# Expert tokens gathered from two rounded parts of the residual instead of three bf16 parts, with four experts in the first gather, in a hybrid decoder layer

## The chip, the cores and the metric

One core of one Trainium2 chip runs the whole layer. The metric is device time in microseconds (us), the median of 3 executions. The lower the better.

## What is computed

One layer: RMSNorm, a mixer (mLSTM heads and S5 groups), the residual x1 = x + mixer, and a mixture of experts, then a last RMSNorm. The change touches the passage from x1 to the experts:

```python
def hierarchical_moe(h, ...):               # h = rmsnorm(x1, norm_ffn_g), 256 tokens x 1024
    g_logits = (t @ rg_w) + rg_b            # 4 groups, top 1
    e_logits = (t @ re_w) + re_b            # 8 experts in that group, top 2
    ...
    for e in range(32):                     # 32 experts, 1024 -> 512 -> 1024
        ye = (silu(t @ w_gate[e]) * (t @ w_up[e])) @ w_down[e]
        y = y + combine[:, e:e + 1] * ye
```

All is float32. The weights of the 32 experts are 201 MB, read once.

## The kernel before

**Instruction order.** The schedule is written out by hand: each engine runs its instructions in the order of the program text, and waits only on semaphores. The engines are PE (TensorE), DVE (VectorE), ACT (ScalarE), POOL (GpSimd) and SP (SyncE, which here only issues DMAs).

**Expert weights.** `fetch(upto)` issues the next loads, 1 MB each (a quarter of the gate, up or down matrices of one pair of experts, 12 loads a pair, 192 in all, in the order of the list `order`). They go into 23 buffers (`NP` = 23, named `half0` to `half22`) that are reused in turn. Until the experts start, these buffers also hold the mixer's weights and scratch. Load number 22 (counted from 0) goes into `half5`, where x1 lies until the router has read it. Load 23 is the first that reuses a buffer of an expert: SP waits at it until the gate matmuls of pair 0 have gone through c = 0 to 3.

**From x1 to the first expert** (L1035 to L1097). x1 is finished in four PSUM pieces (128 tokens `b` by 512 columns `q`). `residual` copies each to SBUF, `squares` sums its squares, `transpose1` transposes it for the router, `logits` multiplies it with the router weights, and `choose` (9 small DVE operations) gives the mask `msk` of each token's two experts. `rank` multiplies the mask with a triangle of ones on PE, which numbers the tokens of each expert, and `onehots` turns the numbers into one-hot columns (`oh`), 64 places for each expert. `warm` issues matmuls whose results nobody reads. `parts_of_x` splits x1 into three bf16 tiles `xp` whose sum is x1; each piece costs two ACT and two DVE operations. `gather_first` multiplies the parts with the one-hots of experts 0 and 1 only, and `gains` scales the result into `xg`, the operand of the experts. In pair 0 (L1109 on) the gate matmuls (`wide`, L1014) follow. Between c = 3 and c = 4 come the factors, the count `cnt` of tokens for the largest expert, and the one-hots of experts 2 and 3, which are gathered after pair 0's up matmuls. Later `gather(range(4))` gathers four experts at a time, in the odd pairs 1 to 13.

**A pair**: gate (8 values of c), Silu on ACT, up (8 values), product on DVE, four transposes (L1152), down, and the scatter of the pair before into four PSUM banks. The last pair's down matrices come in ten smaller loads. At the end ten sums and scalings give the output (from L1202).

**Memory.** `mw`, `cst`, `Sc` and `xall` are tiles of their own. `cap` first holds the causal mask. Once its last reader is done, the final norm's gains are loaded into it on SP's queue (L748), and PE spreads them in pair 14 (L1147).

Of the kernel before, what the change touches and what calls it, by code (L numbers as in the profile page):

```python
# [19 lines left out]
P = 128  # L20
# [52 lines left out]
def tile_hymba(ctx, tc, x, norm_mix_g, w_in, conv_w, conv_b, i_bias, f_bias, mlstm_norm_g,  # L73
# [21 lines left out]
    xall = pool.tile([P, 3072], F32, name="xs")  # L95
    xs = cuts(xall, (2, 1024))[0]
    xp = cuts(xall.bitcast(BF16), (3, 2, 1024))[0]
    Y = pool.tile([P, 2, 512], F32R, name="Y")
    Sc = pool.tile([P, 2, 128], F32R, name="Sc")
    mw = pool.tile([P, 3840], F32, name="mw")  # L100
    ident = pool.tile([P, P], F32, name="ident")
    cst = pool.tile([P, 1584], F32, name="cst")
    PS = pp.tile([P, 8, 512], F32, name="psum")
    (g1, g2, gbias, mask8, mask2, dl16, dlt4, half_pi, neg_half, one, idx, ssq, en, rd, sq, sc, mgh, hb) = cuts(
        cst, 8, 8, 1, 8, 2, 16, 4, 1, 8, 1, 128, 2, (2, 4), (2, 4), (2, 4), (2, 4), 4, 4)
    (lg, gm, tv, msk, m12, rk, wt, el, es, pen, gw, w1, w2, r2, s2, cnt) = cuts(
        cst, (2, 40), (2, 8), (2, 8), (2, 32), (2, 2, 32), (2, 32), (2, 32), (2, 32), (2, 4), (2, 4), 2, 2, 2, 2, 2, 2,
        start=228)
    tri, ones, cap, rbias, rw, rTB, ldt0, sh, wp = cuts(
        cst, 128, 128, 128, 40, (8, 40), 80, 2, (2, 2), 2, start=752)  # L110
    oh = cuts(cst.bitcast(BF16), (2, 4, 64), start=2 * 1176)[0]

    rpt = cuts(cst.bitcast(BF16), (2, 3), start=2 * 1496)[0]
    rtmp, rp = cuts(cst, 2, 2, start=1500)
# [44 lines left out]
    va, pre, La, mr, R = cuts(mw, (2, 4, 129), (4, 256), 256, 256, (2, 4, 128))  # L159
    Gt, Bc, Mx = cuts(smB, 256, 256, 256)  # L160
    K4T, dd2 = cuts(mw, 512, (16, 2, 16))
    hh = cuts(mw, (2, 4, 129), start=2056)[0]
# [541 lines left out]
    zt = cuts(mw, (2, 256), start=3088)[0]  # L704
# [43 lines left out]
    SP.dma_start(cap[0:8], norm_final_g.rearrange("(c n) -> c n", c=8))  # L748
# [102 lines left out]

    x1 = cuts(half(5), (2, 1024))[0]
    LB = (2, 4)

# [48 lines left out]
    def rank(b):  # L903
        rp = PS[:, LB[b], 64:96]
        MM(rp, tri, msk[:, b], start=b == 0, stop=True, skip_group_check=True)
        yield
        STT(rk[:, b], rp, 1.0, msk[:, b], OP.add, OP.mult)
        yield
        onehots(0, (0, 1), (b,))
        yield  # L910
# [25 lines left out]

    def parts_of_factors():
        V.tensor_copy(rpt[:, :, 0], r2)
        TT(rtmp, r2, rpt[:, :, 0], OP.subtract)
        V.tensor_copy(rpt[:, :, 1], rtmp)  # L940
        TT(rpt[:, :, 2], rtmp, rpt[:, :, 1], OP.subtract)
# [3 lines left out]
    xg, act, aT, ow = cuts(mw, (8, 256), 512, (4, 128), (2, 2, 64))  # L945
# [3 lines left out]
    def gather_first(b, steps):  # L949

        for k, q in steps:
            for c in range(4):
                MM(PS[:, DN[q], 128 * c:128 * c + 128], xp[:, k, b, 4 * q + c::8],
                   oh[:, b, 0:2].rearrange("p e s -> p (e s)"), start=c == b == k == 0, stop=b == 1 and k == 2,
                   skip_group_check=True)
            if b and k == 2:
                gains(DN[q], slice(4 * q, 4 * q + 4), slice(0, 128))

    def factors(js, bk):

        at = PS[:, bk, 0:8].rearrange("p (j k) -> p j k", j=2)
        for n, j in enumerate(js):
            for b in range(2):
                MM(at[:, j, 0:3], oh[:, b, 2 * j:2 * j + 2].rearrange("p e s -> p (e s)"), rpt[:, b],
                   start=n == b == 0, stop=b == 1, skip_group_check=True)
        V.tensor_reduce(rp[:, js[0]:js[-1] + 1], at[:, js[0]:js[-1] + 1, 0:3], AX.X, OP.add)

    def gains(bk, cs, ss):
        n, m = cs.stop - cs.start, ss.stop - ss.start
        TT(xg[:, cs, ss], PS[:, bk, :].rearrange("p (c s) -> p c s", c=n), fr(g2[:, cs], (1, n), (0, m)), OP.mult)  # L970

    def onehots(e0, es, bs=(0, 1)):
# [5 lines left out]
    def gather(es):  # L978

        n = 8 // len(es)  # L980
        ss = slice(64 * es[0], 64 * es[-1] + 64)
        m = ss.stop - ss.start
        for f in range(8 // n):
            for c in range(n):
                for b in range(2):
                    for k in range(3):
                        MM(PS[:, DN[f % 2], m * c:m * c + m], xp[:, k, b, n * f + c::8],  # L987
                           oh[:, b].rearrange("p e s -> p (e s)")[:, ss], start=c == b == k == 0, stop=b == 1 and k == 2,
                           skip_group_check=True)
            gains(DN[f % 2], slice(n * f, n * f + n), ss)  # L990
# [45 lines left out]
    sqs, junk1 = cuts(mw, 1024, 512, start=2048)  # L1036
# [3 lines left out]
    next(part[0, 0])  # L1040
    next(part[0, 0])
# [12 lines left out]
    next(part[0, 1])  # L1054
    next(part[0, 1])
# [17 lines left out]
    fetch(NP)  # L1073
    next(part[1, 1])
    next(part[1, 0])
# [4 lines left out]
    logits(1, 1)  # L1080
    run(rank0)
    next(part[1, 1])
# [261 lines left out]
```

## Time and profile before

| what | value |
|---|---|
| median of 3 runs | 608.95 us (608.2 to 609.27) |
| time of the profiled execution | 607.72 us |
| its span | 606.0 us |
| PE busy | 585.0 us, 97% |
| DVE busy | 224.2 us, 37% |
| ACT busy | 127.3 us, 21% |
| POOL busy | 57.5 us, 9% |
| moved by DMA | 219.79 MB, 363 GB/s on average |

The span is the stretch from the first instruction to the last. The profiled execution's own time is 1.72 us longer than it. Busy time of PE is modelled and counts matmuls that overlap as one stretch. PEld is the loading of PE's stationary operand, which overlaps with PE. An f32 matmul shows as two records; an f32r one (f32 data, rounded, one pass) as one, and its weight loads are labelled f32.

### The profile page before, as it was taken

Reading aid. Unit: us, or ns where it says so; the run is one execution under the profiler, and the core shown is the slowest. Engines: PE = TensorE matmul, PEld = TensorE weight load, DVE = VectorE, ACT = ScalarE, POOL = GpSimd, SP = SyncE. Lnnn points to the kernel's source line nnn. Section 1 sums busy time; section 2 is a strip of 40 time slices with the busy share of each in tenths; the row PEclk is TensorE's granted clock in tenths of the full one; section 3 lists DMA queues with packets and bytes.
Section 4 is the critical chain, followed back from the end, with each engine's and each line's share of the span. In section 5 each row is a group of like instructions: output and inputs, shape, how many; then the busy total and the mean of one; then the engine's idle time right before and its main releaser. Section 6 shows DMA issues by size and latency. Waiting matters only on the chain.

```text
span 606.0 us, 8112 instructions
## 1 busy us (share of the span) xinstructions
PE 585.0 (97%) x3228; PEld 312.8 (52%) x3228; DVE 224.2 (37%) x583; ACT 127.3 (21%) x237; POOL 57.5 (9%) x74
## 2 busy tenths in 40 slices
PE   8999999999999999999999999999999999999993
PEld 7788587688543633543363344336334533534352
DVE  5969962886622313221231322123121312222123
ACT  4483547624201010000101010010101011001023
POOL 7040319131000000000000000000000000000003
PEclk9999999999999999999999999999999999998998
DMA  8792239679999999999999999999999999999992
GB/s 228 232 302 77 69 136 415 254 293 420 384 407 421 418 420 420 420 420 419 419 419 417 422 419 419 422 417 422 418 418 421 416 422 417 421 420 417 420 309 76
DMA packets 51337, 219.79 MB, mean 363 GB/s; under 512 B 15236, under 2 KB 20448, under 8 KB 27232
## 3 DMA queue, kind: packets, MB, share of 16 engines
q1 hardware_dynamic: 50800, 218.17, 89.9%
q10 hardware_dynamic: 496, 1.06, 0.5%
q8 instruction: 27, 0.44, 0.3%
q14 instruction: 14, 0.11, 0.0%
HBM read 218.17 MB, written 1.05 MB: 362 GB/s over the span
## 4 chain that ended last, share of the span: by engine, by line
PE 46%; DMA 40%; DVE 6%; issue 4%; ACT 2%; POOL 1%; POOLq 0%; SPq 0%; DVEq 0%; ACTq 0%
PE psum L1014 25%; DMA half<-in_expert_w_down_dram 13%; DMA half<-in_expert_w_gate_dram 13%; DMA half<-in_expert_w_up_dram 13%; PE psum L431 4%; PE psum L803 4%; PE psum L987 3%; PE psum L1029 2%; DVE mw L533 2%; DMA xs<-in_x_dram 1%; POOL half L421 1%; PE psum L1152 1%; PE psum L1033 1%; PE psum L810 1%; PE psum L461 1%
## 5 line engine op out<-in xcount | busy, mean ns | idle before, releaser
L1014 PE MATMUL psum<-half,mw 128*64 128x512 f32 x1504 | 334.0, 596 | 4.0 <-ACT mw L1154 1.5
L1014 PEld LDWEIGHTS psum<-half,mw 128*64 128x64 f32 x1504 | 106.4, 137 | 210.0 <-issue 193.6
L1021 DVE SCALAR_TENSOR_TENSOR Y<-psum,cst,Y 128x512 fp32r<-128x512 f32 x28 | 21.0, 751 | 125.5 <-ACT Y L1020 125.5
L1138 DVE SCALAR_TENSOR_TENSOR mw<-psum,cst,mw 128x512 f32<-128x512 f32 x16 | 12.0, 751 | 145.0 <-PE psum L1014 145.0
L1020 ACT ACTIVATE Y<-psum,cst 128x512 fp32r<-128x512 f32 x28 | 19.2, 687 | 189.1 <-PE psum L1014 126.9
L431 PE MATMUL psum<-half,half 128*128 128x256 f32 x192 | 42.6, 380 | 0.4 <-DVE half L281 0.4
L987 PE MATMUL psum<-cst,xs 128*128 128x256 bf16 (+1 forms) x384 | 40.9, 267 | 0.0
L1179 POOL MEMSET mw<- 128x2 f32 x1 | 0.1, 99 | 424.2 <-PE psum L1152 424.2
L987 PEld LDWEIGHTS <-xs 128*128 128x128 bf16 x384 | 40.0, 144 | 0.0
L431 PEld LDWEIGHTS psum<-half,half 128*128 128x128 f32 x192 | 36.1, 190 | 5.7 <-DVE half L281 0.6
L1029 PE MATMUL psum<-Y,Sc 128*128 128x512 f32 x112 | 33.6, 422 | 0.0
L1029 PEld LDWEIGHTS psum<-Y,Sc 128*128 128x128 f32 x112 | 18.8, 188 | 25.2 <-issue 22.7
L421 POOL TENSOR_TENSOR half<-half,half 128x1024 fp32r<-128x1024 f32 x10 | 24.6, 2481 | 59.2 <-ACT half L420 38.7
L1154 ACT COPY mw<-psum 128x256 f32<-128x256 f32 x15 | 5.6, 372 | 111.5 <-PE psum L1152 111.5
L970 DVE TENSOR_TENSOR mw<-psum,cst 128x512 f32<-128x512 f32 x32 | 22.0, 691 | 15.0 <-PE psum L987 13.1
L803 PE MATMUL psum<-half,half 128*128 128x512 f32 x96 | 24.2, 402 | 0.3 <-ACT half L831 0.3
L1131 ACT ACTIVATE mw<-psum,cst 128x512 f32<-128x512 f32 x16 | 11.0, 687 | 52.9 <-PE psum L1014 52.9
L803 PEld LDWEIGHTS psum<-half,half 128*128 128x128 f32 x96 | 17.5, 188 | 4.6 <-ACT half L831 0.5
L995 DVE TENSOR_SCALAR mw<-cst 128x64 f32<-128x64 f32 x64 | 15.6, 308 | 0.0
L439 PE MATMUL psum<-half,half 128*128 128x512 f32 x32 | 13.9, 592 | 0.0
L1152 PE MATMUL psum<-ident,mw 128*128 128x128 f32 x64 | 11.8, 308 | 1.9 <-DVE mw L1138 1.9
L1154 DVE COPY mw<-psum 128x256 f32<-128x256 f32 x15 | 6.4, 425 | 19.0 <-ACT mw L1154 19.0
(348 smaller groups left out, 510.2 us busy)
## 6 DMA issues: line engine op xcount, KB each, us to landing
half<-in_expert_w_gate_dram SPq DMA_DIRECT2D x64, 1024.0 KB, 19.9
half<-in_expert_w_up_dram SPq DMA_DIRECT2D x64, 1024.0 KB, 19.9
half<-in_expert_w_down_dram SPq DMA_DIRECT2D x60, 1024.0 KB, 19.9
half<-in_w_in_dram SPq DMA_DIRECT2D x8, 1024.0 KB, 7.9
half<-in_w_out_dram SPq DMA_DIRECT2D x4, 1024.0 KB, 8.3
half<-in_expert_w_down_dram SPq DMA_DIRECT2D x6, 512.0 KB, 13.7
half<-in_w_in_dram SPq DMA_DIRECT2D x4, 512.0 KB
half<-in_expert_w_down_dram SPq DMA_DIRECT2D x4, 256.0 KB, 7.2
```

The source lines that it names most:

```text
L421: es[i].tensor_tensor(rests[i], w, made[i].bitcast(F32), OP.subtract)
L431: MM(PS[:, bk + m // 2, 256 * (m % 2):256 * (m % 2) + 256], w[:, at:at + 128], flat(h32, c), start=c == 0 and m % 2 == 0, stop=c == 7, ski ...
L439: MM(PS[:, bks[b], :], h32[:, c, b], raw[g, c // 2][:, 512 * (c % 2):512 * (c % 2) + 512], start=c == 0, stop=c == 7, skip_group_check=True)
L803: MM(PS[:, WB[2 * b + i], :], m[:, k % 4, ts], w[:, 512 * i:512 * i + 512], start=False, stop=n == 7 and m is ml, skip_group_check=True)
L970: TT(xg[:, cs, ss], PS[:, bk, :].rearrange("p (c s) -> p c s", c=n), fr(g2[:, cs], (1, n), (0, m)), OP.mult)
L987: MM(PS[:, DN[f % 2], m * c:m * c + m], xp[:, k, b, n * f + c::8], oh[:, b].rearrange("p e s -> p (e s)")[:, ss], start=c == b == k == 0, ...
L995: TS(ow[:, b, e], places, rk[:, b, 2 * pr + e:2 * pr + e + 1], wt[:, b, 2 * pr + e:2 * pr + e + 1], OP.is_equal, OP.mult)
L1014: MM(PS[64 * e:64 * e + 64, bk, 0:w[e].shape[-1]], lhs[:, c, 64 * e:64 * e + 64], w[e], start=c == 0, stop=c == n - 1, skip_group_check=True)
L1020: ACT(hi, src, AF.Copy, scale=w)
L1021: STT(lo, src, w, hi.bitcast(F32), OP.mult, OP.subtract)
L1029: MM(PS[:, WB[2 * b + n], :], Sc[:, b], Y[:, k], start=False, stop=False, skip_group_check=True)
L1152: TR(PS[:, GB, 128 * c:128 * c + 128], act[:, c::4], ident)
```

## The change

- `parts_of_x` makes two parts instead of three: x1 rounded to f32r (ACT copy) and the rest as f32r (DVE subtraction), both read from x1 in SBUF. They are the tiles `xp[0]` (in the memory of `xs`) and `xp[1]` (in that of `more`, a new scratch tile that also takes over parts of `mw`).
- `oh` becomes two f32r tiles, one for each block of 128 tokens, each with four experts. They take the memory of the router weights `rw` and of `tri` and `ones`. `onehots` is one DVE operation of 256 columns for a block, instead of one of 64 columns for each expert.
- `gather` uses 256 columns throughout, two parts instead of three (f32r instead of bf16). The first gather already has all four experts: half of its columns (f = 0, 1) in two steps by block, the other half (f = 2, 3) for both blocks at once, all ahead of pair 0. The gather in pair 0 is gone.
- The count `cnt` moves ahead of pair 0: its two matmuls with `msk` stand after `choose(1)`, with four `warm` matmuls behind them in place of the six. `fetch(NP)` (load 22) moves from behind `transpose1(1, 1)` to behind the second `rank`.
- `rpt` has two f32r parts, `Sc` takes the memory of `cap`, and the final norm's gains are loaded on ACT's queue in pair 14 instead of on SP's earlier.

```diff
+    xs = cuts(shared("xs", 2048), (2, 1024))[0]
+    more = shared("more", 2048)
-    mw = pool.tile([P, 3840], F32, name="mw")
+    mw = pool.tile([P, 3072], F32, name="mw")
...
+    tri, ones = cuts(shared("tri", 256), 128, 128)
+    cap, rbias, rTB, ldt0, sh = cuts(shared("cap", 256), 128, 40, 80, 2, (2, 2))
+    rw = cuts(shared("rw", 320), (8, 40))[0]
...
-    SP.dma_start(cap[0:8], norm_final_g.rearrange("(c n) -> c n", c=8))
...
     def parts_of_x(b, q):
-        cs, t = slice(512 * q, 512 * q + 512), sqs[:, 512 * q:512 * q + 512]
-        r, src = xp[:, :, b, cs], PS[:, WB[2 * b + q], :]
-        A.copy(r[:, 0], src)
-        yield
-        TT(t, src, r[:, 0], OP.subtract)
-        yield
-        A.copy(r[:, 1], t)
-        yield
-        TT(r[:, 2], t, r[:, 1], OP.subtract)
+        cs = slice(512 * q, 512 * q + 512)
+        A.copy(xp[0][b][:, cs], x1[:, b, cs])
+        yield
+        TT(xp[1][b][:, cs], x1[:, b, cs], xp[0][b][:, cs].bitcast(F32), OP.subtract)
         yield
...
+    def gather(fs, bks, bs=(0, 1)):
+        for f, bk in zip(fs, bks):
+            for c in range(2):
+                for b in bs:
+                    for k in range(2):
+                        MM(PS[:, bk, 256 * c:256 * c + 256], xp[k][b][:, 2 * f + c::8],
+                           oh[b].rearrange("p e s -> p (e s)"), start=c == b == k == 0, stop=b == k == 1,
+                           skip_group_check=True)
+            if 1 in bs:
+                cs = slice(2 * f, 2 * f + 2)
+                TT(xg[:, cs], PS[:, bk, :].rearrange("p (c s) -> p c s", c=2), fr(g2[:, cs], (1, 2), (0, 256)), OP.mult)
...
+    def onehots(e0, bs=(0, 1)):
         for b in bs:
-            for e in es:
-                TS(oh[:, b, e], places, rk[:, b, e0 + e:e0 + e + 1], None, OP.is_equal)
+            TT(oh[b], fr(places, (0, 4), (1, 64)), fr(rk[:, b, e0:e0 + 4], (1, 4), (0, 64)), OP.is_equal)
...
     transpose1(1, 1)
-    fetch(NP)
     next(part[1, 1])
     next(part[1, 0])
-    next(part[1, 0])
     warm(3, DN[0])
     rank0 = rank(0)
     next(rank0)
     logits(1, 1)
+    oh[0] = cuts(shared("rw", 320, F32R), (4, 64))[0]
     run(rank0)
-    next(part[1, 1])
     next(part[1, 1])
     rank1, ch = rank(1), choose(1)
     next(ch)
-    gather_first(0, ((0, 0), (0, 1), (1, 0), (1, 1), (2, 0), (2, 1)))
+    gather((0, 1), DN, (0,))
     MM(PS[:, LB[1], 64:96], ones, msk[:, 0], start=True, stop=False, skip_group_check=True)
     run(ch)
-    next(part[1, 0])
-    warm(6, LB[0])
+    for b in range(2):
+        MM(PS[:, LB[0], 128:160], ones, msk[:, b], start=b == 0, stop=b == 1, skip_group_check=True)
+    warm(4, LB[0])
     next(rank1)
+    oh[1] = cuts(shared("tri", 256, F32R), (4, 64))[0]
     run(rank1)
-    next(part[1, 1])
-    gather_first(1, ((0, 0), (0, 1), (1, 0), (1, 1), (2, 0), (2, 1)))
+    fetch(NP)
+    Sc = cuts(shared("cap", 256, F32R), (2, 128))[0]
+    gather((0, 1), DN, (1,))
+    V.tensor_reduce(cnt[:, 0:1], PS[:, LB[0], 128:160], AX.X, OP.max)
+    V.tensor_copy(cnti[:, 0:1], cnt[:, 0:1])
+    gather((2, 3), (4, 3))
     parts_of_factors()
...
             if c == 3 and pr == 0:
-                factors((0,), DN[0])
-                for b in range(2):
-                    MM(PS[:, DN[1], 0:32], ones, msk[:, b], start=b == 0, stop=b == 1, skip_group_check=True)
-                V.tensor_reduce(cnt[:, 0:1], PS[:, DN[1], 0:32], AX.X, OP.max)
-                V.tensor_copy(cnti[:, 0:1], cnt[:, 0:1])
-                onehots(0, (2, 3))
+                factors(DN[1])
                 scatter_weights(0)
         ACT(act, PS[:, GB, :], AF.Silu, scale=rp[:, pr % 2:pr % 2 + 1])
+        if pr == 14:
+            ng, a15, rows = cuts(half(tag(169)), 1024, (4, 128), 128)
+            A.dma_start(rows[0:8], norm_final_g.rearrange("(c n) -> c n", c=8))
...
-        if pr == 0:
-            gather((2, 3))
-            factors((1,), GB)
-        elif pr % 2 and pr < 14:
-            gather(range(4))
-            factors((0, 1), GB)
+        if pr % 2 and pr < 14:
+            gather(range(4), 2 * DN)
+            factors(GB)
```

## Rows read from the trace of the kernel before

**Rows 1.** The page: clock, DMA share and rate, span in 40 slices.
```profile
PEclk9999999999999999999999999999999999998998
DMA  8792239679999999999999999999999999999992
GB/s 228 232 302 77 69 136 415 254 293 420 384 407 421 418 420 420 420 420 419 419 419 417 422 419 419 422 417 422 418 418 421 416 422 417 421 420 417 420 309 76
```

**Rows 2.** Chain of waits: start us, us, what; first and last DMA piece.
```profile
278.65 19.84 DMA half<-in_expert_w_gate_dram
...
499.62 19.88 DMA half<-in_expert_w_up_dram
```

**Rows 3.** Timeline of PEld: start, us, operation; in brackets its idle time, releaser.
```profile
519.54 0.20 PEld L1014 LDWEIGHTS psum<-half,mw 128*64 128x64 f32 x4 [2.22 <-DMA half<-in_expert_w_up_dram]
...
549.47 2.34 PEld L1014 LDWEIGHTS psum<-half,mw 128*64 128x64 f32 x13 [0.51 <-DMA half<-in_expert_w_up_dram]
...
579.47 0.20 PEld L1014 LDWEIGHTS psum<-half,mw 128*64 128x64 f32 x4 [0.81 <-DMA half<-in_expert_w_down_dram]
```

**Rows 4.** Timeline of SP's queue: issues of expert loads around pair 0's start.
```profile
148.95 0.96 SPq L150 DMA_DIRECT2D half<-in_expert_w_down_dram  x2
161.32 0.33 SPq L150 DMA_DIRECT2D half<-in_expert_w_down_dram  x1
```

**Rows 5.** Windows: busy of each engine, PEclk, DMA share, GB/s.
```profile
84.00:161.00 77.00, 74.45 (x533) 58.37 (x531) 48.02 (x128) 39.20 (x77) 27.09 (x20) 1.00 0.87 350
...
162.00:163.00 1.00, 1.00 (x6) 0.32 (x6) 0.93 (x8) 0.00 (x0) 0.00 (x0) 1.00 0.94 188
```

**Rows 6.** Chain of waits from the last router matmuls into pair 0's gate.
```profile
150.60 0.90 PE psum L876 x8
...
153.16 1.42 PE psum L901 x12
154.57 0.16 PE psum L905 x2
...
155.45 1.42 PE psum L953 x20
...
156.89 0.70 DVE mw L970
...
157.64 3.65 PE psum L1014 x16
```

**Rows 7.** Timeline of DVE: the second block's choice.
```profile
151.21 0.68 DVE L930 TENSOR_TENSOR mw<-psum,xs 128x512 f32<-128x512 f32 x1
151.81 0.25 DVE L879 SCALAR_TENSOR_TENSOR cst<-psum,cst 128x40 f32<-128x40 f32 x1
...
153.78 0.19 DVE L896 TENSOR_TENSOR cst<-cst 128x32 f32<-128x32 f32 x1
```

**Rows 8.** DVE groups by shape: busy, mean ns, idle before.
```profile
L725 DVE TENSOR_TENSOR half<-half,half 128x256 fp32r<-128x256 f32 x4 | 1.7, 426 | 1.9 <-ACT half L724 1.9
```

**Rows 9.** Timeline of PEld: f32r loads with 256 columns; f32 loads of stride 8.
```profile
6.73 1.32 PEld L262 LDWEIGHTS psum<-ident,xs 128*128 128x128 f32 x10
...
588.70 0.53 PEld L1033 LDWEIGHTS psum<-half,half 128*128 128x128 f32 x4 [0.38 <-issue]
```

**Rows 10.** Lines by source: minimum, median and maximum ns of one.
```profile
L1033 PEld LDWEIGHTS psum<-half,half x20: 186/188/189, 584.8 to 594.3; 128*128 128x128 f32 x20
```

**Rows 11.** Chain of waits: one gather of four experts, in pair 13.
```profile
525.07 5.24 PE psum L987 x48
```

**Rows 12.** DMA issues: queue, count, KB each, median us to landing.
```profile
half<-in_expert_w_gate_dram SPq DMA_DIRECT2D x64, 1024.0 KB, 19.9
...
cst<-in_norm_mix_g_dram ACTq DMA_DIRECT2D x1, 4.0 KB, 5.8
```

**Rows 13.** Timeline in pair 14: Silu, and the matmuls that need the final gains.
```profile
545.60 0.69 ACT L1131 ACTIVATE mw<-psum,cst 128x512 f32<-128x512 f32 x1 [3.13 <-PE psum L1014]
...
554.17 2.05 PE L1147 MATMUL psum<-cst,ident 8*128 8x128 f32 x16
```

More of the change, by code (lines that the diff above doesn't have):

```diff
@@ L158, in tile_hymba @@
     x1_, x2_ = cuts(mw, (16, 16), (16, 16))
-    va, pre, La, mr, R = cuts(mw, (2, 4, 129), (4, 256), 256, 256, (2, 4, 128))
+    va, pre, La, mr = cuts(mw, (2, 4, 129), (4, 256), 256, 256)
+    R = cuts(more, (2, 4, 128))[0]
     Gt, Bc, Mx = cuts(smB, 256, 256, 256)
     K4T, dd2 = cuts(mw, 512, (16, 2, 16))
-    hh = cuts(mw, (2, 4, 129), start=2056)[0]
+    hh = cuts(more, (2, 4, 129))[0]
     xv = x[0].rearrange("(b p) f -> b p f", p=P)
@@ L703, in tile_hymba @@
     tO = fr(yg, (512, 2), (1, 512))
-    zt = cuts(mw, (2, 256), start=3088)[0]
+    zt = cuts(more, (2, 256), start=1032)[0]
     for h in range(2):
@@ L850, in tile_hymba @@
     sqs = cuts(mw, 1024, start=2048)[0]
+    junk1 = cuts(mw, 512, start=2048)[0]
     x1 = cuts(half(5), (2, 1024))[0]
     LB = (2, 4)
+    xp = [cuts(shared(tag, 2048, F32R), 1024, 1024) for tag in ("xs", "more")]
     def residual(b, q):
@@ L908, in rank @@
         yield
-        onehots(0, (0, 1), (b,))
+        onehots(0, (b,))
         yield
@@ L938, in parts_of_factors @@
         V.tensor_copy(rpt[:, :, 0], r2)
[L939 to L945, printed above, removed]
+        TT(rpt[:, :, 1], r2, rpt[:, :, 0].bitcast(F32), OP.subtract)
+    xg, act, aT = cuts(mw, (8, 256), 512, (4, 128))
     places = idx[:, 1:65]
     GB, UB, DN = 2, 4, (3, 6)
[L949 to L957, printed above, removed]
@@ L959, in factors @@
-    def factors(js, bk):
-        at = PS[:, bk, 0:8].rearrange("p (j k) -> p j k", j=2)
-        for n, j in enumerate(js):
-            for b in range(2):
[L964 to L970, printed above, removed]
@@ new lines, in factors @@
+    def factors(bk):
+        at = PS[:, bk, 0:4].rearrange("p (j k) -> p j k", j=2)
+        for j in range(2):
+            for b in range(2):
+                MM(at[:, j], oh[b][:, 2 * j:2 * j + 2].rearrange("p e s -> p (e s)"), rpt[:, b],
+                   start=j == b == 0, stop=b == 1, skip_group_check=True)
+        V.tensor_reduce(rp, at, AX.X, OP.add)
+    def onehots(e0, bs=(0, 1)):
+        for b in bs:
+            TT(oh[b], fr(places, (0, 4), (1, 64)), fr(rk[:, b, e0:e0 + 4], (1, 4), (0, 64)), OP.is_equal)
@@ L1039, in tile_hymba @@
     squares(0, 0, V)
-    next(part[0, 0])
-    next(part[0, 0])
     for n in range(6, 8):
@@ L1114, in tile_hymba @@
         if pr % 2 and pr < 14:
-            onehots(2 * pr + 2, range(4))
+            onehots(2 * pr + 2)
         for c in range(8):
@@ L1141, in tile_hymba @@
         if pr == 14:
-            ng, a15 = cuts(half(tag(169)), 1024, (4, 128))
             S1 = cuts(half(tag(172), F32R), (2, 2, 128))[0]
@@ L1180, in tile_hymba @@
     junk = cuts(mw, (3, 256))[0]
-    Yl = cuts(mw, (2, 128), start=3072)[0]
+    Yl = cuts(mw, (2, 128), start=768)[0]
     def last_down(k):
@@ L1280, in tile_hymba @@
                         for b in range(2):
-                            for k in range(3):
-                                MM(PS[:, q, 128 * c:128 * c + 128], xp[:, k, b, 4 * q + c::8], o1[:, b],
-                                   start=b == k == 0, stop=b == 1 and k == 2, skip_group_check=True)
+                            for k in range(2):
+                                MM(PS[:, q, 128 * c:128 * c + 128], xp[k][b][:, 4 * q + c::8], o1[:, b],
+                                   start=b == k == 0, stop=b == k == 1, skip_group_check=True)
                     TT(xo[:, 4 * q:4 * q + 4], PS[:, q, :].rearrange("p (c s) -> p c s", c=4),
@@ L1286, in tile_hymba @@
                 for b in range(2):
-                    MM(PS[:, 4, 256:259], o1[:, b], rpt[:, b], start=b == 0, stop=b == 1)
-                V.tensor_reduce(rp[:, 0:1], PS[:, 4, 256:259], AX.X, OP.add)
+                    MM(PS[:, 4, 256:258], o1[:, b], rpt[:, b], start=b == 0, stop=b == 1)
+                V.tensor_reduce(rp[:, 0:1], PS[:, 4, 256:258], AX.X, OP.add)
                 for bk, w in ((2, wgt), (3, wup)):
```

47 lines of the change are left out of this document (15 added, 32 removed).

## The prediction, made before the kernel with the change had run

> **What bounds the kernel now.** PE's busy share of 97% suggests that PE is the bound, so the slices of the span come first [rows 1]. The reader is to see there that the DMA engines are full (tenths of 9, 407 to 422 GB/s) in every slice from 136 us to 576 us but one, that of 151 to 167 us, with 384. The 201 MB of expert weights at 420 GB/s alone take 479 us. Then the chain of waits: between 278.65 and 519.5 us it runs through twelve DMA pieces of about 19.9 us, one behind the other [rows 2]. Last the weight loads of PE: it waits for expert data at 519.54 us, and twice more near the end, at 549.47 and 579.47 us [rows 3]. The last of these waits is for pair 14's down weights, and what follows (rest of pair 14, pair 15, final norm) is a fixed 26.5 us of work. So the stream of expert loads sets the end. PE works off a store of 23 loads at its own pace, and has used it up by 519.5 us; that it is busy all the time does not make it the bound.
>
> A change of PE's or DVE's work therefore moves the end in one way only: by making the stream idle for a longer or a shorter time. Where does the stream idle? After 136 us at one place, in that slice. Loads 21 and 22 are issued at 148.95 us, load 23 only at 161.32 us, when pair 0's gate has gone through its first half and freed a buffer [rows 4]. The 23 loads ahead of it and three mixer weights are 26 x 1.0486 = 27.26 MB; from 84 us, where I take the queue as empty, to 161 us the DMA moved 77 us x 350 GB/s = 26.95 MB [rows 5]. The last 0.31 MB take 0.7 us, so the stream runs dry at about 161.7 us. In the next microsecond but one it moves at 188 GB/s instead of 420 [rows 5]: load 23 came just in time to cost little. Whatever delays the first half of pair 0's gate is from here on lost one for one, and nothing gives it back, since the stream is already at its full rate afterwards.
>
> **The change, part by part: the way to pair 0's gate.** In the chain [rows 6] the second block's router matmuls (L876) end at 151.50, the gate (L1014) starts at 157.64, and its first half takes 3.65 us to 161.29. I take 151.50 for the changed kernel too: DVE loses four operations in parts_of_x before it, but PE is the engine that sets it (a gain of 0.1 us is possible).
>
> *First step, the choice of the second block.* Before, the block-0 one-hots are small and DVE reaches L879 at 151.81, with the subtraction L930 (start to start 0.60) hidden in the wait for the router matmuls [rows 7]. Now the one-hot tile lies in the memory of the router weights, so DVE must wait for these matmuls to end before it writes it (151.50, and 0.05 for the semaphore). An operation of 256 columns to f32r takes 0.43 [rows 8], and then the last subtraction of parts_of_x stands ahead of L879: 0.60. L879 starts at 151.55 + 0.43 + 0.60 = 152.58, that is 0.77 later, or 0.67 with the possible 0.1. I take +0.7. The choice itself is unchanged (2.16 us from L879 to the end of L896 [rows 7]). Queued behind the waiting one-hot on DVE are this subtraction and the choice; for the choice waits the rank, for that the gather.
>
> *Second step, the rank.* Before, the mask is there at 153.97, PE is still in the warm matmuls until 154.57 and the rank is done at 154.73: 0.76 later [rows 6, 7]. In the new order the count matmul of block 1 waits for this mask, and all four warm matmuls stand behind it, ahead of the rank. These are 2 + 8 records of 0.12 us (1.42 us for twelve [rows 6]) = 1.2 us, then the rank, 0.05 + 0.35: about 1.6 us. That is +0.8.
>
> *Third step, number and one-hot.* From the rank's end to the gather it was 155.45 - 154.73 = 0.72 [rows 6], with two one-hots; one of 0.43 takes their place. +0.
>
> *Fourth step, the gather.* Before, 24 short matmuls and the first scaling stand between 155.45 and 157.64: 2.19 us [rows 6]. Now 8 matmuls (f = 0, 1, block 1) and 16 (f = 2, 3, both blocks) stand ahead of the gate in PE's order, all of 256 columns in f32r. The trace has no such gather; the price of one matmul lies between 0.114, the distance of weight loads where four such matmuls with contiguous weights follow each other ((0.53 - 0.19) / 3 [rows 9, 10]), and 0.19, a whole weight load with nothing overlapped [rows 10]. Weights of stride 8 in f32, as here, load 0.126 apart in the first transposes ((1.32 - 0.19) / 9 [rows 9]), which is the nearest row: 24 x 0.126 + 0.05 = 3.07, +0.9 (bounds 2.79 and 4.6: +0.6 to +2.4). The scalings are hidden: the gate's first two values of c need only the first, done long before the last matmul of the gather.
>
> The Trainium skill speaks against this part (SBUF — State Buffer, the section on the DMA port swizzle): SBUF is read in lines of 16 bytes, each access to a new line pays, and the free stride ends at 4 fp32 or 8 bf16 elements. By it the old gather (stride 8 in bf16) reads freely and the new one (stride 8 in f32) does not. The rows above show a penalty of that kind only as 0.126 against 0.114; if it were large, the sum would go to the upper bound.
>
> Sum: 0.7 + 0.8 + 0 + 0.9 = 2.4 us later for the gate's first half, with bounds 1.5 (0.1 us off each step, and the one-hot wait hidden down to 0.4) and 3.9. Load 23 goes out at about 163.7, and the stream stands still 2.4 us longer.
>
> **The rest.** *Load 22* waits for the last subtraction from x1 (about 152.6) instead of 149; the queue then has 23 - 1 loads' worth until 161.7 - 2.5 = 159.2 us, so its cover is 6 us and the cost nothing. *Pair 0's second gather* is gone: PE reaches the down matmuls sooner than the gate's delay, so no second gap opens. *Later gathers*: 32 x 0.126 = 4.0 us instead of 5.24 [rows 11], seven times, all on an engine that waits for the stream in the end: nothing. *DVE and ACT* (fewer one-hots and casts) are off the path: nothing. *L748* is a small issue on SP ahead of a long wait: nothing. *The gains on ACT's queue* go out after the Silu of pair 14 ends at 546.3 and are needed at 554.17 [rows 13]: a cover of 7.9 us. A 4 KB load on ACT's queue took 5.8 us beside busy queues; the upper bound is 19.9, the time of a load that stands behind SP's others [rows 12]. I take 5.8: hidden. *Earlier memory moves* (mw, more) touch only operations that are long done: nothing.
>
> Against the profiled execution's own 607.72 us that is 607.72 + 2.4 = 610.1; the median of the runs stands 1.2 us above it, so 608.95 + 2.4 = 611.35 us (+0.4%).
>
> **The rivals.**
> *A, the stream does not feel it.* If the gap at 162 us is not an empty queue but a start-up effect, the delay costs under 1.2 us: 609 to 610. For it: the DMA share stays at 0.94 in the slow microsecond [rows 5]. Against it: the bytes add up to an empty queue. 0.17.
> *B, PE decides the end, so it is not slower.* From 519.5 us on the chain runs on PE, whose DMA waits there are small: 0.51 and 0.81, and part of these is no real wait [rows 3]. If PE's work from there sets the end, the one gather in that stretch gives 1.2 us: 608.95 - 1.2 = 607.7. It decides if the data of 579.47 would have been there 1.2 us earlier and the gate's delay is under 0.5 us. Against it: the delay of the stream is larger than PE's whole slack. 0.09.
> *C, dear weight loads.* 0.19 for each of the 24: +3.9, 612.9. 0.09.
> *D, late gains.* They land after 19.9 us, at 566: PE stands 12 us in pair 14, about 608.95 + 2.4 + 11.5 = 622.9. 0.03. The Trainium skill (DMA: Bandwidth & Descriptors, Queues, rings and completion order) says that each DMA engine takes turns between the queues it has work for, by packets; that would keep ACT's load from standing behind SP's and lowers this chance, but no row shows it at full load.
> *E, the clock falls.* PE stands idle about 1.2 us before the second mask and 0.7 before the gather; the granted clock was full through such a gap of 0.7 in the trace [rows 1, 6]. At half clock the gather and half a gate cost about 6.5 us more: 618. 0.04.
>
> **Numbers.** The forecast (+1.2 to +3.3) has 0.58. With the two slow rivals and C, and a little of the forecast's low end taken off, slower by over 0.2% (1.2 us, about what a measurement of this kernel can tell from no change) has 0.70. A gives most of the 0.21 for no change; B gives 0.09 for faster. The likeliest time is 611.3. The range takes in A and most of B below and C above, 608.2 to 613.6, and leaves out D, E and a larger gain.
>
> **What would show it.** In the new trace: L879's second run starts about 0.7 us later; warm matmuls lie between the second mask and the rank; the gate starts at about 160.0; load 23 is issued at about 163.7; the DMA rate stays under half of 420 for 3 to 4 us after 162; every slice after that is full; the wait for pair 14's down weights is there again, 2.4 us later. If the gate starts later but the DMA shows no longer gap, A holds; if the last 60 us show no wait for data, B. The prediction is wrong if the gate starts by 158.5, or if the stream before 150 us is packed otherwise than now.

## The result and the profile after

625.17 us median (624.52 to 626.12, four runs) against 608.58 (608.18 to 609.27, four runs): ratio 1.0268, 95% interval 1.0248 to 1.0289. The change costs 16.6 us, and the predicted 611.3 with its range up to 613.6 is far off. The profiled execution has a span of 624.4 us against 606.0.

The page of the changed kernel, slices of 15.6 us, answers to [rows 1]:

```profile
PEclk9999999999799999999999999999999999999898
DMA  8890158699599999999999999999999999997951
GB/s 223 253 313 25 67 195 345 270 358 419 206 408 418 421 419 420 420 419 419 417 420 420 420 419 419 419 420 420 419 420 418 420 418 420 419 419 309 394 154 70
```

Two differences: the hole in the stream of loads near 160 us is deeper (206 GB/s in that slice, where it was 384), with a lower granted clock beside it, and the stream thins out over the last four slices (309, 394, 154, 70 GB/s) where before only the last two were low (309, 76). The chain of waits, shares of the span by engine, says what took its place; in the kernel before it read PE 46%, DMA 40%:

```profile
PE 85%; DVE 6%; issue 4%; ACT 2%; POOL 1%; DMA 1%; POOLq 0%; DVEq 0%; ACTq 0%
```

TensorE now sets the end from pair 0 on. Its weight loads' waits for data (engine, line, what was waited for: us in total, times, longest) say the same. Before they add up to 6.2 us, and with the change to 2.7, none longer than 0.4:

```profile
PEld psum L1014 <- DMA half<-in_expert_w_up_dram: 4.2, 5, 2.2
PEld psum L1014 <- DMA half<-in_expert_w_down_dram: 1.4, 3, 0.8
PEld psum L1014 <- DMA half<-in_expert_w_gate_dram: 0.6, 2, 0.3
```

and with the change:

```profile
PEld psum L999 <- DMA half<-in_expert_w_down_dram: 1.4, 5, 0.3
PEld psum L999 <- DMA half<-in_expert_w_gate_dram: 0.9, 3, 0.3
PEld psum L999 <- DMA half<-in_expert_w_up_dram: 0.4, 1, 0.4
```

What makes TensorE slower stands in the chain, start us and us, on the way to pair 0's gate (L999) and in pair 13; it answers to [rows 6] and [rows 11]:

```profile
151.83 0.42 DVE rw L975
152.26 0.60 DVE more L937
152.86 0.18 DVE cst L887
...
154.75 0.20 DVE cst L904
...
155.00 0.64 PE psum L1069 x2
155.64 1.87 PE psum L909 x8
157.50 0.28 PE psum L913 x2
...
158.60 6.14 PE psum L956 x24
164.75 3.79 PE psum L999 x16
...
543.64 7.71 PE psum L956 x32
```

The reader is to see three things. The gate starts at 164.75 instead of 157.64. The first gather's 24 matmuls take 6.14 us. And a gather of four experts with 32 matmuls takes 7.71 us where 48 took 5.24: 0.241 us for each matmul, at full clock (the first gather ran at a granted 0.50, see below). The loads of its weights, by source line (minimum, median and maximum ns), against 188 in [rows 10]:

```profile
L956 PEld LDWEIGHTS psum<-rw,xs x64: 312/338/344, 152.3 to 550.1; 128*128 128x128 f32 x64
```

One mark in each pair, the transposes of `act` on TensorE's timeline, adds it up. Before, in pairs 0, 1, 13 and 15:

```profile
173.31 0.75 PE L1152 MATMUL psum<-ident,mw 128*128 128x128 f32 x4 [0.96 <-DVE mw L1138]
...
200.22 0.74 PE L1152 MATMUL psum<-ident,mw 128*128 128x128 f32 x4
...
524.15 0.70 PE L1152 MATMUL psum<-ident,mw 128*128 128x128 f32 x4
...
574.36 0.75 PE L1152 MATMUL psum<-ident,mw 128*128 128x128 f32 x4 [0.92 <-DVE mw L1138]
```

and with the change:

```profile
180.48 0.75 PE L1134 MATMUL psum<-ident,mw 128*128 128x128 f32 x4 [0.96 <-DVE mw L1121]
...
204.77 0.72 PE L1134 MATMUL psum<-ident,mw 128*128 128x128 f32 x4
...
542.69 0.73 PE L1134 MATMUL psum<-ident,mw 128*128 128x128 f32 x4
...
595.35 0.75 PE L1134 MATMUL psum<-ident,mw 128*128 128x128 f32 x4 [0.93 <-DVE mw L1121]
```

Pair 0 is 7.2 us late. Pair 1 is 4.6 late: pair 0's second gather is gone. By pair 13 it is 18.5: six gathers of 2.8 us more each (the gather itself 2.5, the factors' matmuls and their start the rest) are 16.7, less 2.7 in which the old kernel had by then waited for data. The seventh gather makes it 21.0. From there the old kernel still loses 1.2 in its last waits, and the first transfer of the output is issued 19.8 us later (618.58 against 598.76). The span is only 18.4 longer: the output lands sooner (the last two experiments). The medians differ by 16.6, since the old profile was 0.9 below its median and the new one 1.0 above. Each mark is from one profile, and one profile differs from the next before the change acts: the second block's router matmuls end between 151.1 and 153.3 us in the profiles of this case.

### The profile page after: what moved, and what is told of

It is laid out like the page before. It is cut to its first block, busy times and chain, and to the rows that moved or that the text cites. A ratio compares the mean times of both kernels' runs of the same rounds, so it can differ in the third digit from the quotient of the medians.

```text
span 624.4 us, 7694 instructions
## 1 busy us (share of the span) xinstructions
PE 604.6 (97%) x3048; PEld 332.8 (53%) x3048; DVE 216.8 (35%) x528; ACT 125.3 (20%) x233; POOL 57.9 (9%) x74
## 4 chain that ended last, share of the span: by engine, by line
PE 85%; DVE 6%; issue 4%; ACT 2%; POOL 1%; DMA 1%; POOLq 0%; DVEq 0%; ACTq 0%
PE psum L999 54%; PE psum L956 10%; PE psum L1014 5%; PE psum L439 4%; PE psum L810 4%; DVE mw L541 2%; PE psum L1134 2%; DMA xs<-in_x_dram 1%; POOL half L429 1%; PE psum L1018 1%; PE psum L817 1%; PE psum L469 1%; PE psum L500 1%; PE psum L884 1%; ACT mw L1136 0%
## 5 line engine op out<-in xcount | busy, mean ns | idle before, releaser
L999 PE MATMUL psum<-half,mw 128*64 128x512 f32 x1504 | 331.7, 597 | 2.4 <-ACT mw L1136 1.7
L999 PEld LDWEIGHTS psum<-half,mw 128*64 128x64 f32 x1504 | 105.4, 137 | 207.3 <-issue 197.9
L439 PEld LDWEIGHTS psum<-half,half 128*128 128x128 f32 x192 | 36.1, 190 | 5.7 <-DVE half L289 0.6
L1014 PE MATMUL psum<-Y,cap 128*128 128x512 f32 x112 | 33.6, 422 | 0.0
L1014 PEld LDWEIGHTS psum<-Y,cap 128*128 128x128 f32 x112 | 18.8, 188 | 25.3 <-issue 22.7
L956 PE MATMUL psum<-rw,xs 128*128 128x256 f32 x64 | 26.7, 417 | 0.5 <-DVE rw L975 0.5
L956 PE MATMUL psum<-tri,xs 128*128 128x256 f32 x64 | 26.3, 411 | 0.8 <-DVE tri L975 0.8
L956 PE MATMUL psum<-tri,more 128*128 128x256 f32 x64 | 26.1, 408 | 0.0
L956 PE MATMUL psum<-rw,more 128*128 128x256 f32 x64 | 26.0, 406 | 0.0
L956 PEld LDWEIGHTS psum<-tri,xs 128*128 128x128 f32 x64 | 21.6, 338 | 0.9 <-issue 0.9
L956 PEld LDWEIGHTS psum<-rw,xs 128*128 128x128 f32 x64 | 21.5, 335 | 0.6 <-DVE rw L975 0.6
L956 PEld LDWEIGHTS psum<-rw,more 128*128 128x128 f32 x64 | 21.7, 339 | 0.0
```

The source lines that it names most:

```text
L439: MM(PS[:, bk + m // 2, 256 * (m % 2):256 * (m % 2) + 256], w[:, at:at + 128], flat(h32, c), start=c == 0 and m % 2 == 0, stop=c == 7, ski ...
L956: MM(PS[:, bk, 256 * c:256 * c + 256], xp[k][b][:, 2 * f + c::8], oh[b].rearrange("p e s -> p (e s)"), start=c == b == k == 0, stop=b == k ...
L999: MM(PS[64 * e:64 * e + 64, bk, 0:w[e].shape[-1]], lhs[:, c, 64 * e:64 * e + 64], w[e], start=c == 0, stop=c == n - 1, skip_group_check=True)
L1014: MM(PS[:, WB[2 * b + n], :], Sc[:, b], Y[:, k], start=False, stop=False, skip_group_check=True)
```

## The experiments

The first theory was that loads of f32r weights with a stride of eight elements (32 bytes) are dear, and that f32r itself is not. The rivals: f32r loads are dear at any stride; the gains' late load holds up the stream; the fall of the clock around 160 us makes the damage. The gains were a suspect through this row of the changed kernel, waits of SP's queue:

```profile
SPq L157 <- DMA half<-in_norm_final_g_dram: 16.8, 1, 16.8
```

SP's queue of expert loads stands still for 16.8 us until the gains have landed. Their load is issued on the other queue at 567.18 us, behind pair 14's Silu, and expert loads that could have gone at 552 wait for it. The trace names only what ended the wait. That the loads of both queues take their completion semaphores in turn from a common set, so that a late load holds up those whose turn comes after it, is inferred.

**Contiguous parts.** The changed kernel with the parts stored so that the 128 columns of one weight lie next to each other; ACT and VectorE do the reordering as they write.

```diff
-        A.copy(xp[0][b][:, cs], x1[:, b, cs])
...
+        js = slice(64 * q, 64 * q + 64)
+        src = x1[:, b, cs].rearrange("p (j c) -> p c j", c=8)
+        hi, lo = [xp[k][b].rearrange("p (c j) -> p c j", c=8)[:, :, js] for k in range(2)]
+        A.copy(hi, src)
...
+        TT(lo, src, hi.bitcast(F32), OP.subtract)
...
-                        MM(..., xp[k][b][:, 2 * f + c::8], ...
+                        MM(..., xp[k][b][:, 128 * (2 * f + c):128 * (2 * f + c) + 128], ...
```

> Edit: the two parts of x1 are written so that the 128 columns of one gather matmul lie side by side (stride 1 instead of 8); all else as in the changed kernel. Stride theory (the weight loads of stride 8 in f32r make the gathers slow, and PE thereby the bound): a gather of 32 matmuls falls from 7.7 us to 3.7 to 4.1, PE is ahead of the stream again, the time falls to 611 to 617 us (what stays is the late start and the stop of the stream at 554 to 569 us). f32r theory (an f32r matmul of 256 columns costs 0.24 us whatever its weights' layout): the gather stays at 7.7 us, the time at 625. Gains theory (the stop of the expert loads behind the late load of the final gains sets the time, PE does not): the gather gets faster, the time stays above 620.

611.72 us (611.42 to 612.05), ratio to before 1.0051 (1.0033 to 1.007): 13.5 of the 16.6 us are gone. Loads by source line:

```profile
L959 PEld LDWEIGHTS psum<-rw,xs x64: 186/188/330, 152.3 to 533.9; 128*128 128x128 f32 x64
```

188 ns, as in [rows 10], with 0.115 us from one matmul to the next. TensorE waits for data again (16.5 us in all). The stride is the cause of these 13.5 us, and f32r as such is not. The 330 ns are loads of the first gather, which ran at half clock here too.

**Gains early.** The changed kernel with the gains loaded on SP's queue ahead of load 8, into a tile of their own.

```diff
+    SP.dma_start(fin[0:8], norm_final_g.rearrange("(c n) -> c n", c=8))
     fetch(8)
...
-            A.dma_start(rows[0:8], norm_final_g.rearrange("(c n) -> c n", c=8))
```

> Edit: the final norm's gains are loaded on SP's queue early, as in the kernel before, into a tile of their own (128 more floats per partition, taken from the DMA scratch); all else as in the changed kernel. Stride theory: the stop of the expert loads at 554 to 569 us is gone, but PE is the bound there and the time stays within 1.5 us of 625. Gains theory: the time falls by 8 us or more, to 617 or below.

625.89 us (625.43 to 627.32), ratio 1.0292 (1.027 to 1.0315): no gain. The stop of 16.8 us is real and costs nothing where TensorE is the bound.

**Warm matmuls first.** The changed kernel with the four warm matmuls ahead of the counts, so that TensorE does not idle before them.

```diff
+    warm(4, LB[0])
     for b in range(2):
         MM(PS[:, LB[0], 128:160], ones, msk[:, b], ...)
-    warm(4, LB[0])
```

> Edit: the four warm matmuls stand ahead of the two count matmuls instead of behind them; all else as in the changed kernel. If the place of the warm matmuls costs what I take it to (about 1 us at full clock on the way to the rank, and the clock's fall to half behind the idle wait for the second mask): the granted clock stays at 1.0 from 154 to 165 us, the gate starts 3 to 6 us earlier (159 to 162 us), and since PE is the bound the time falls by as much, to 619 to 622. Rival (the clock falls all the same, or the start is hidden by the stream): gate start 1 us earlier at most, time 624 to 625.

625.37 us (624.89 to 625.56), ratio 1.0274 (1.0255 to 1.0293). The expectation missed. The clock fell all the same, only later, to 0.57 between 160 and 164 us, and the gate came at 164.48. In this profile the router matmuls ended at 153.25 instead of 151.79, so the way from them to the gate took 11.2 us instead of 13.0. The time shows nothing of it.

**All three together.**

> All three edits together: contiguous parts, gains early, warm matmuls ahead of the counts. Stride theory: nothing but a start later by 0 to 1.5 us is left, the stream of expert loads sets the end, 607 to 610.5 us. If f32r or the larger first gather as such were the cost: above 615. Gains theory alone: as in its own run, no gain from the other two edits.

609.13 us (608.08 to 610.53), ratio 1.0011 (0.9998 to 1.0025). The clock stays at 1.00 from 150 to 174 us, and the gate starts at 159.71, where the prediction had 160.0. On SP's and PEld's timelines, load 23 and the wait that answers to the first of [rows 3] at 519.54:

```profile
163.39 0.33 SPq L158 DMA_DIRECT2D half<-in_expert_w_down_dram  x1
```

```profile
521.61 0.20 PEld L1004 LDWEIGHTS psum<-half,mw 128*64 128x64 f32 x4 [2.22 <-DMA half<-in_expert_w_up_dram]
```

Both are 2.07 us late: with the stride out of the way, the stream carries the gate's delay on to TensorE's first wait, as predicted. The contiguous kernel alone had half clock from 156 to 162 us and its gate at 163.50, 3.8 us later. The first gather's last 24 matmuls make 1.7 of these (4.68 us there, 2.99 here); the rest is the place of the warm matmuls and their clock, which no run tells apart. 2.6 us show in the time.

**What a stride costs.** The changed kernel, each odd pair's gather with another stride.

```diff
-                        MM(..., xp[k][b][:, 2 * f + c::8], ...
+                        MM(..., xp[k][b][:, slice(2 * f + c, 2 * f + c + 127 * st + 1, st)], ...
-            gather(range(4), 2 * DN)
+            gather(range(4), 2 * DN, st={1: 8, 3: 1, 5: 2, 7: 3, 9: 4, 11: 5, 13: 6}[pr])
```

> The changed kernel, with the gathers of pairs 1, 3, 5, 7, 9, 11 and 13 reading weight columns 8, 1, 2, 3, 4, 5 and 6 elements apart (the tokens gathered are then mixed up from pair 3 on; the number and size of the matmuls stay). Theory, that a load costs by the 16-byte lines that its 128 columns touch (4 fp32 to a line, so 32, 64, 96 and from 4 on 128 lines): stride 1 as in the contiguous kernel (188 ns, 0.115 us apart), 2 and 3 between, 4, 5, 6 and 8 all at 338 ns and 0.241 us. Rival one, any stride over 1 costs all: 338 ns from 2 on. Rival two, it grows on to 8: 4 to 6 below 338 ns. Time by the theory about 617 us, by the first rival 621.

One run, 614.49 us, where the theory had 617. The loads by source line, pairs 1 to 13 in order, so strides 8, 1, 2, 3, 4, 5, 6:

```profile
L956 PEld LDWEIGHTS psum<-rw,xs x8: 313/339/345, 204.5 to 211.3; 128*128 128x128 f32 x8
...
L956 PEld LDWEIGHTS psum<-rw,xs x8: 186/188/190, 260.8 to 264.5; 128*128 128x128 f32 x8
...
L956 PEld LDWEIGHTS psum<-rw,xs x8: 193/196/200, 313.5 to 317.2; 128*128 128x128 f32 x8
...
L956 PEld LDWEIGHTS psum<-rw,xs x8: 252/262/267, 366.6 to 371.5; 128*128 128x128 f32 x8
...
L956 PEld LDWEIGHTS psum<-rw,xs x8: 309/331/332, 420.7 to 427.3; 128*128 128x128 f32 x8
...
L956 PEld LDWEIGHTS psum<-rw,xs x8: 295/318/321, 476.8 to 483.1; 128*128 128x128 f32 x8
...
L956 PEld LDWEIGHTS psum<-rw,xs x8: 302/321/325, 532.6 to 538.9; 128*128 128x128 f32 x8
```

From stride 4 on the load costs its full 320 to 340 ns; stride 3 costs 262, stride 2 almost nothing. The first rival falls; of the second's growth there are some 20 ns between strides 5 and 8. The rule that the prediction quoted from the Trainium skill (SBUF — State Buffer, the section on the DMA port swizzle) agrees in its lines of 16 bytes and in wanting two accesses to a line for full speed: stride 2 has two fp32 in a line, stride 4 one. Its figure of a free stride of 4 fp32 does not agree: 4 already costs all.

**The same in bf16**, in the kernel before, by the same edit with strides 8, 1, 2, 3, 4, 5, 7.

> The kernel before, with its bf16 gathers of the same pairs reading weight columns 8, 1, 2, 3, 4, 5 and 7 elements apart (tokens mixed up from pair 3 on). In its own trace these loads at stride 8 take 143 ns, against 97 ns for the one-hots' contiguous bf16 loads (L964), while the matmuls follow each other at 0.109 us either way. Theory, that bf16 pays for lines as fp32 does and before hid it behind the 256 columns that each weight is used for: about 97 ns at stride 1, more from stride to stride, 143 at 8, and no change of spacing or of the time (608). Rival, that bf16 loads do not care: 143 ns at all of them.

One run, 607.48 us. Strides 8, 1 and 4 by source line:

```profile
L987 PEld LDWEIGHTS <-xs x48: 140/143/148, 201.0 to 206.1; 128*128 128x128 bf16 x48
...
L987 PEld LDWEIGHTS <-xs x48: 97/98/98, 254.5 to 259.6; 128*128 128x128 bf16 x48
...
L987 PEld LDWEIGHTS <-xs x48: 111/114/117, 415.1 to 420.2; 128*128 128x128 bf16 x48
```

The bf16 load gets dearer with the stride too (143 against 98 ns), but nothing follows from it: all seven gathers took 5.4 us on TensorE's timeline, 0.109 us from one matmul to the next. The f32r load of 338 ns spreads its matmuls from 0.115 to 0.241 us. That the shorter load is hidden behind the 256 columns of the matmul before it, and the longer one is too long for that, is inferred.

**TensorE's slack.** The kernel before with the gathers' loss put on TensorE by other means.

```diff
+            warm(11, DN[0])
             gather(range(4))
```

> The kernel before, with eleven extra 128-column matmuls (11 x 0.237 = 2.6 us) ahead of each of the seven gathers of the odd pairs: what the strided loads cost the changed kernel (7.71 - 5.24 = 2.5 us each), put on TensorE with nothing else changed. Theory, that before's TensorE has only the few us of slack that its waits for DMA show (about 6 us in all) and loses the rest: 7 x 2.6 = 18.2 less some 4 to 6, so 620 to 623 us, with the waits for DMA gone from the trace. Rival, that the weight stream sets the end and these gathers hide behind it as the prediction had it: 608.2.

620.78 us (619.93 to 622.98), ratio 1.0217 (1.0191 to 1.0242). The eleven take 2.45 us each time, 17.2 in all; 12.8 of them reach the time, and the waits for data shrink to 0.4 us at most. What the stream could hide was 4 to 5 us.

**The stream, one for one.** The kernel before with nothing but a later gate.

```diff
-    gather_first(1, ((0, 0), (0, 1), (1, 0), (1, 1), (2, 0), (2, 1)))
+    gather_first(1, ((0, 0), (0, 1)))
+    warm(9, LB[0])
+    gather_first(1, ((1, 0), (1, 1), (2, 0), (2, 1)))
```

> The kernel before, with nine extra 128-column matmuls (0.237 us each by the spacing of L901's, together 2.1 us) in the middle of the second half of its first gather, and nothing else: pair 0's gate and load 23 come 2.1 us later, at about 159.8 and 163.4. By the prediction's rule that a late stream reaches the end one for one: about +2.1 us, 610.3 us at before's 608.2. The rival, that the stream's lateness is partly made up before the end (the changed kernel with all three repairs was 2.1 us late in the stream and 0.9 us in the time): +0.9, about 609.1. That the stream does not feed the end: 608.2.

609.31 us (608.41 to 611.71), ratio 1.0022 (1.001 to 1.0035), so +0.6 to +2.1 us. In the trace load 23 is 2.0 us late (163.33), the mark of pair 13 is 2.1 late (526.28), and the spans differ by 2.3. The traces favour the one-for-one rule; the times are compatible with it at the interval's end and do not settle it against a smaller share.

**A better version.** On top of the three repairs: the first one-hots in `Y`'s memory, so that they do not wait for the router matmuls; the last subtraction behind the second block's choice; rank ahead of the counts; most of the gather of f = 2, 3 behind the gate's first half.

```diff
-    oh[0] = cuts(shared("rw", 320, F32R), (4, 64))[0]
+    for b in range(2):
+        oh[b] = Y[:, b, 0:256].rearrange("p (e s) -> p e s", e=4)
...
     run(ch)
+    next(part[1, 1])
     warm(4, LB[0])
     next(rank1)
...
     gather((0, 1), DN, (1,))
-    gather((2, 3), (4, 3))
+    gather((2,), (4,), halves=(0,))
...
             if c == 3 and pr == 0:
+                gather((2,), (4,), halves=(1,))
+                gather((3,), (3,))
```

> The kernel with all three repairs, with more taken from the way to pair 0's gate: the first one-hots written to Y's memory, so that they do not wait for the router matmuls (0.5 us); the last difference of the parts behind the second block's choice instead of ahead of it (1.2 us, of which about 0.4 come back ahead of the ranks); rank ahead of the counts (0.3 us); the gather of the last four column chunks of x but one quarter behind the gate's first half (1.4 us). Gate at about 157.1 instead of 159.71 (before: 157.64), load 23 at about 160.8. By the stream 2.6 us less than the repaired kernel and about 0.5 less than before: 607.7. The rival, that the repaired kernel's lateness hardly reached the end: about 608.2 to 609, no better than before.

605.62 us (604.9 to 607.71), ratio 0.9961 (0.9946 to 0.9975): faster than both. The expected 607.7 was for the stream alone. Load 23 goes out at 161.70 (expected 160.8), 1.7 us sooner than with the three repairs but 0.4 later than before, and the output is issued at 598.6, as before (598.76). In this profile, though, the router matmuls end at 152.44 instead of 151.50; from there to the gate it is 5.6 us, against 6.1 before and 8.1 with the three repairs. So some 0.5 us of its lead of 2.3 over the old kernel may be won in the stream, which this profile cannot show; the 1.5 us between the spans are the shorter landing of the output, below.

**The subtraction on GpSimd.** The same with one edit.

```diff
-        TT(lo, src, hi.bitcast(F32), OP.subtract)
+        (G.tensor_tensor if b and q else TT)(lo, src, hi.bitcast(F32), OP.subtract)
```

> As the run before it, but the last difference of the parts runs on GpSimd at its old place instead of on VectorE behind the choice. If GpSimd takes under 2.5 us for 128x512 and does not slow VectorE: ranks 0.4 us earlier, gate at about 156.8, load 23 at 160.5, 607.4 us. If it takes longer or slows VectorE's operations beside it, the ranks or the gather wait: gate at 158 or later, 608.5 us or more.

605.70 us (605.01 to 606.7), ratio 0.9955 (0.994 to 0.997): no different. From the router matmuls to the gate it took 5.8 us (5.6 in the run before). GpSimd took 1.65 us, and one of VectorE's operations beside it 0.77 us instead of 0.16.

**The output's landing.** In all profiles of the old code the output's transfer on SP landed after 3.5 to 4.2 us, in those with the change after 2.3, with the same tiles and sizes. The DMA queues of the last 12 us, packets, MB and share, before:

```profile
q8 instruction: 2, 0.03, 1.3%
q14 instruction: 3, 0.02, 0.5%
...
out_dram<-half SPq DMA_DIRECT2D x2, 256.0 KB, 4.2
```

and in the better version:

```profile
q8 instruction: 1, 0.02, 0.6%
q14 instruction: 2, 0.02, 0.3%
...
out_dram<-half SPq DMA_DIRECT2D x2, 256.0 KB, 2.3
```

The change has 180 matmul records less. Two runs give the better version back its old length of code:

```diff
+            for n in range(12 + (pr > 1)):
+                MM(PS[:, DN[0], 0:2], ident, ident[:, 0:2], start=True, stop=True)
             gather(range(4), 2 * DN)
```

> The best kernel so far, with 90 two-column fp32 matmuls ahead of the odd pairs' gathers, so that TensorE has 3228 matmul records again, as in the kernel before (3048 without). They take some 0.06 us each, 0.8 us a gather, which TensorE's waits for DMA (15 us in that kernel) cover. What is asked is the end: the output's transfer on SP's queue landed after 4.2, 4.0, 4.0 and 3.5 us in the four profiles of before's code (before and its three variants) and after 2.3 us in all seven with the change, and in before's last 10 us there is one packet more on each of the two instruction queues. Theory, that the length of TensorE's code puts a load of code beside the output: it lands after 3.5 to 4.2 us again, three packets of the one instruction queue in the last 10 us or two instead of one, and the time is 1 to 2 us longer than 605.6, about 607. Rival, that it is something else in the change: 2.3 us, 605.7.

and, in the second, 55 copies of two columns on VectorE as well:

> As the run before it, and with 55 two-column copies more on VectorE, so that it too has as many instructions as in the kernel before (583; 528 without), hidden behind pairs in which it is mostly idle. If it is VectorE's code, or both engines' together, that puts a load of code beside the output: 2.3 us and 605.7 in the run before it, and 3.5 to 4.2 us and about 607 here. If code has no part in it: 2.3 us and 605.7 in both.

Landing after 4.3 and 3.9 us, with two packets on the first instruction queue in both. The first:

```profile
q8 instruction: 2, 0.03, 1.4%
q14 instruction: 2, 0.02, 0.3%
...
out_dram<-half SPq DMA_DIRECT2D x2, 256.0 KB, 4.3
```

Longer code on TensorE alone brings the slow landing back, in one profile of each kernel. The times, 618.48 us (ratio 1.0166, 1.014 to 1.0192) and 615.90 (1.0145, 1.01 to 1.0191), missed the expected 607 by 11.5 and 8.9 us: a two-column matmul in fp32 is two records of 0.114 us and not 0.06 us together, so each gather got 2.7 us longer, and it is the run on TensorE's slack once more. On top of that the granted clock fell behind some of these narrow matmuls (0.72 from 256 to 262 us in both runs, 0.57 from 424 to 430 us in the first); by the marks of the odd pairs this cost the first run 5.9 us and the second 2.8.

## Why the prediction failed

*What bounds the kernel.* Right for the kernel before. Wrong in the step that follows from it, that a change of TensorE's work can move the end only through the hole in the stream. TensorE was close behind: 17.2 us more of its work cost 12.8.

*First step, the choice.* +0.7 forecast; the mask came 1.0 later (154.96 against 153.97). Of this 0.3 stands ahead of the step: the router matmuls ended at 151.81 and not at 151.50. The step itself was right.

*Second step, the rank.* +0.8 forecast, +2.1 measured: the order was right, but the warm matmuls ran at half clock (1.87 us for eight records, where [rows 6] have twelve in 1.42). The granted clock was 0.50 from 156 to 164 us. Rival E named the fall with a chance of 0.04, behind an idle wait of 1.2 us for the second mask. The wait was 0.21 us, for the strided first half of the gather kept TensorE busy until 154.4 us. The clock fell in it, at 154.9. What makes it fall is not shown: the kernel with the gains early has the same order and the same wait, and kept full clock until 160.8 us; with contiguous weights alone TensorE stood idle 1.28 us before the mask, and the clock fell behind that. With contiguous weights and the warm matmuls ahead it did not fall. The rows are two windows of the changed kernel (busy of each engine, PEclk, DMA share, GB/s), and the wait on PEld's timeline there and with the gains early:

```profile
154.00:156.00 2.00, 1.90 (x11) 1.78 (x11) 0.84 (x5) 0.00 (x0) 0.00 (x0) 0.72 1.01 418
156.00:158.00 2.00, 1.77 (x10) 1.63 (x8) 0.19 (x1) 0.00 (x0) 0.00 (x0) 0.50 1.03 426
```

```profile
155.00 0.50 PEld L1069 LDWEIGHTS psum<-cst,tri 128*128 128x128 f32 x2 [0.21 <-DVE cst L904]
...
156.20 0.30 PEld L1071 LDWEIGHTS psum<-cst,tri 128*128 128x128 f32 x2 [0.21 <-DVE cst L906]
```

*Third step.* +0.1 for 0.

*Fourth step, the gather.* This is the step that failed: "Weights of stride 8 in f32, as here, load 0.126 apart in the first transposes, which is the nearest row: 24 x 0.126". It was 0.241, and the gather cost +4.0 instead of +0.9. With contiguous weights it cost +0.8 at full clock and +2.5 where the clock was half for most of it. At either clock 24 x 0.241 = 5.8 us lies past the upper bound of 4.6. The row was of transposes, and these load faster than f32r matmuls at each stride that the traces have (1, 4 and 8). The same trace shows what a stride does to them, had contiguous ones been set beside strided ones; loads by source line, the first transposes (stride 8, the row of the forecast), those of x1 (stride 1) and of `act` (stride 4):

```profile
L262 PEld LDWEIGHTS psum<-ident,xs x16: 185/189/226, 5.6 to 7.9; 128*128 128x128 f32 x16
...
L871 PEld LDWEIGHTS psum<-ident,half x16: 138/140/143, 142.4 to 149.2; 128*128 128x128 f32 x16
...
L1152 PEld LDWEIGHTS psum<-ident,mw x64: 195/212/222, 173.3 to 574.7; 128*128 128x128 f32 x64
```

The upper bound, 0.19, was a contiguous load's duration and so bounded nothing. Rival C had the mechanism, with this bound and for the 24 first matmuls only.

*Later gathers.* "32 x 0.126 = 4.0 us instead of 5.24, seven times, ... nothing" fell with the same price: seven times 2.5 us more, beyond the 4 to 5 us of slack. This is the greater part of the loss. Without the stride the forecast's own mechanism is left: with all three repairs, gate, load 23 and stream are 2.1 us late for the 2.4 forecast. That the sums agree so well is partly luck: the choice was 1.2 later there (0.4 of it the reordering), the rank 0.1 sooner, since the warm matmuls had been moved out of its way, and the gather cost 0.8.

*The gains.* Forecast hidden behind Silu. They held up SP's queue for 16.8 us instead, as inferred above by a semaphore shared with the expert loads, which no step had; with TensorE as the bound it cost nothing.

*Not foreseen.* The output landing after 2.3 us instead of 3.5 to 4.2. In the one profile of the kernel with all three repairs, the output is issued 1.85 us later than before and the span is only 0.5 longer. This is the likely reason that its time shows +0.9 us and not +2.1.

## What to carry to other kernels

Price a matmul by its weight load whenever the weights' layout or type changes, from a row of the same kind of matmul at the same stride, and check by the distance of such matmuls whether the load is still hidden. "Hidden" has a size: before a cost is put at nothing because another resource sets the end, add up the waits that the covered engine really has (6.2 us here, of which 4 to 5 could be used) and compare the change summed over all its repetitions. Store a part in the order in which it will be read as weights; reordering it while it is written cost 0.4 us on the path, once.

## What was not expected of the hardware

- A strided f32r load does not follow TensorE's clock: 312 to 345 ns at full clock and, in the first gather at a granted 0.50, 315 to 345. A contiguous one takes 188 ns at full and 330 at half clock. So most of the price of the stride is paid at full clock: from one matmul to the next it was 0.241 us against 0.115 there, and 0.243 against 0.213 at half clock.
- Code is loaded by the DMA engines too (the page lists two instruction queues), and the length of TensorE's code decided whether one more load of it fell into the last 12 us, beside the last transfer, which then landed after 3.5 to 4.3 us instead of 2.3. That the load's own traffic delays it is inferred. The Trainium skill (Runtime: NRT & Kernel Launch, Instruction fetch mechanics) has code fetched in blocks of 16 KiB; the pages of both kernels agree (27 packets with 0.44 MB before, 25 with 0.41 after on the first instruction queue).
